# Order of weight turns, stores and the last plain block in a hybrid encoder block (attention, state space layer, two FFNs) on one core

## The chip, the core and the metric

The kernel runs on one core of a Trainium2 chip. Its engines are TensorE (PE, matrix products; PEld is its weight load), VectorE (DVE), ScalarE (ACT), GpSimd (POOL) and SyncE (SP), which here only issues DMAs. The metric is the device time of one execution in microseconds; lower is better.

## The reference

One layer over 1024 tokens of width 1024: a half-weighted SwiGLU FFN, a mixer with neighbourhood attention and a bidirectional state space layer side by side, a second FFN, a gated per-layer embedding and a last norm. All data is float32.

```python
h = h + 0.5 * swiglu(rms_norm(h, ffn1_norm), wg1, wu1, wd1)            # 1024 -> 2816 -> 1024
u = rms_norm(h, mix_norm);  z = u @ w_in                               # q | k | v | s_in | gates
y_attn = neighbourhood_attention(q, k, v, na_rpb) @ w_attn_out         # 8 heads of 64, window 8 x 16
y_ssm = s5_branch(s_in, lam, log_dt, b, c, d, glu_w, glu_b) @ w_ssm_out
g_attn, g_ssm = split(sigmoid(gates), 2)
h = h + (g_attn * y_attn + g_ssm * y_ssm) @ w_out
h = h + 0.5 * swiglu(rms_norm(h, ffn2_norm), ...)
h = h + (p @ w_ple) * sigmoid(rms_norm(h, ple_norm) @ w_ple_gate)
return rms_norm(h, final_norm)

def s5_branch(...):                # 32 groups of 16 channels, 64 complex states each
    y = d_skip * u + scan_forward(u) + scan_backward(u)
    y = gelu(y)
    return y * sigmoid(y @ glu_w + glu_b)
```

## The kernel before

**Products.** Every large product is made of three matmuls on rounded halves: an operand is split into a high part (an ACT cast, L151) and a low part (a DVE subtraction, L152), and `mm3` (L182 to L184) adds high x high, high x low and low x high. Weights come by DMA as 128x512 blocks (`hbuf`, `wblk`, `wgs`), and their split is `wh`, `wl` (in the GLU `wgh`, `wgl`). "Turned" below is said of the attention weights: the scaled scores `sm` are transposed on PE before they meet the values.

**FFN1** uses a scheme of seven products for the four quadrants (class `Seven`). The hidden units are handled in pairs of blocks. Pair 0 is computed plainly (items "C"; matmuls at L657): its four results are evacuated by `evac_plain`, which multiplies by the norm's scale `rs`. The last of them, block 21, is kept back in `late` and finished by `finish_plain`. The pairs 1 to 10 are items ("A", pair, product, gate or up): 7 products x 2, of 12 matmuls each; `evac_a` moves the results `gz`, `uz`, `gx` and so on from PSUM with ACT copies (L577), DVE additions (L581) and an ACT Silu (L585). When a pair has its four blocks, `combine` makes four sums of them (DVE, L534 to L540), and what stage B needs is stored in `a_d`. Stage B, items ("B", product, pair), reads it back as `araw`, splits it into `ah`, `al` and multiplies by `wblk`.

**The side generator.** While FFN1 runs, a generator advances by one tick every three matmuls. `gen_params` loads the parameters of the state space layer (`g_prm`, L775) into the pool `gp` and works them out on DVE. Then for each of 16 pairs of groups `gen_pair` lets POOL build the tables `gm` and `em`, and 25 ticks later `gen_pair_products` turns `gm` on PE (`tp`), multiplies `em` by `bd` (`kp`), copies `kp` into `ka` and stores to DRAM: `fm` to `f_d`, and pieces of `ka` and `em` to `e_d`. `begun` is what opens the way: it ends the hand-written order for DVE and ACT, closes the pool `up` that held the norm's scales, and opens `gp` in its memory.

**The mixer.** After the projections of v, q and k, attention runs in 64 units (8 heads x 2 row blocks x 4 column blocks), one per step `j`. A step computes the scores of unit j (`attn_scores`: PE `s`, DVE addition of the bias table `tb` and row minimum, ACT exponential L1208, DVE reciprocal L1209, ACT scaling L1210), turns the `sm` of unit j-2 (`attn_turn`, PE `pt`, then `pth`, `ptl`) and multiplies unit j-4 by its values (`attn_values`, `O`). Between steps PE works on the gates' projection (`gt`). From step 48 (`SO`) on, one pair of the state space output starts in each step: `ssm_out` loads `emi` from `e_d` and `u_d`, and copies the states into `xs`; three steps later its matmuls `yo` follow. Then comes the GLU: `glu_out(m, t)` for two halves t of the tokens and four blocks m of the weights.

**What sets the order.** The order on PE is written out by hand for the whole kernel, that on DVE and ACT until `begun`. The rest, with POOL and SP, is put in order by a scheduler when the program is built; each engine then works through its queue in order, SP's DMA issues too. Most tiles of 128x512 of the mixer (`sm`, `pth`, `ptl`, `vhl`, `emi`, the GLU's weight halves) share one pool of 56 buffers.

Of the kernel before, what the change touches and what calls it, by code (L numbers as in the profile page):

```python
# [8 lines left out]
F32 = mybir.dt.float32  # L9
# [7 lines left out]
P = 128  # L17
# [4 lines left out]
NH = 8  # L22
GRID = 64
L = 8
NCH = SEQ // L
# [13 lines left out]
def encoder_block(ctx, tc, I, out):  # L39
# [396 lines left out]
    class Ffn:  # L436
# [118 lines left out]
        def evac_plain(self, c, g, o):  # L555
            x, r = self.hid.setdefault(0, {}), self.seven.rs[int(c[0]) - 1]
            if g == 0:
                x[c] = tmp("c" + c)
                V.tensor_tensor(x[c], o, r, ALU.mult)
                A.activation(x[c], x[c], AF.Silu)  # L560
                return
            V.tensor_tensor(x[c], o, x[c], ALU.mult)
            V.tensor_tensor(x[c], x[c], r, ALU.mult)
            if c != "21":
                self.out(0, "a" + c, x[c])
            else:
                self.combine(0, x, tmp("s1"), tmp("s2"), tmp("s4"))

        def evac_a(self, p, i, g):
            z = self.hid.setdefault(p, [{}, {}])[g]  # L570
# [127 lines left out]
        def run(self):  # L698
# [4 lines left out]
            for n, item in enumerate(items):  # L703
# [186 lines left out]
    def gen_pair(pr):  # L890
# [35 lines left out]

        cmul(em, tg, "pe", L + 1, bc, (0, 1))
        load_bc(pr + 1)
        for g in range(2):
            for r in range(2):  # L930
                for d in range(2):
                    n0 = 1 - d
                    nc.sync.dma_start(e_d[2 * pr + g, r * 64:(r + 1) * 64, (1 + d) * P:(2 + d) * P],
                                      em[g * 64:(g + 1) * 64, r, d, n0:n0 + L].rearrange("p n o -> p (n o)"))
# [6 lines left out]
    def gen_pair_products(pr, gm, em, bd):  # L941
# [20 lines left out]
        A.copy(ka[:, 128:240], kp[0:32, 144:256])  # L962
        V.tensor_tensor(ka[:, 112:128], ka[:, 112:128], kp[0:32, 128:144], ALU.add)
        V.scalar_tensor_tensor(ka[:, 112:128], gen["dm"], gen["dk"][:, pr:pr + 1], ka[:, 112:128], ALU.mult, ALU.add)
        for s in range(L):
            nc.sync.dma_start(e_d[2 * pr:2 * pr + 2, s * 16:(s + 1) * 16, 0:P],
                              ka[:, (L - 1 - s) * 16:(L - 1 - s) * 16 + P])


    f_cm = tc.tile_pool(name="f1", bufs=1)  # L970
# [128 lines left out]
    def ssm_out(pr):  # L1099
# [8 lines left out]
        xs = tw("xs", [P, 2, 2, NCH], F32)  # L1108
        for g in range(2):
            for r in range(2):  # L1110
                for d in range(2):
                    sd = Xv[g * 64:(g + 1) * 64, r, pr, d * (NCH + 2):d * (NCH + 2) + NCH]
                    (A.copy if g == r else V.tensor_copy)(xs[r * 64:(r + 1) * 64, g, d], sd)

        def go():
            o = bank("yo")
# [48 lines left out]
    def load_v(hd, cb):  # L1165
# [7 lines left out]
        V.tensor_tensor(hl[0:n, :, 1], vf[0:n], hl[0:n, :, 0].bitcast(F32), ALU.subtract)  # L1173
        vld[hd, cb] = hl

    def make_tabs(hd, rb):
        bt = ap_.tile([P, 12, 32], F32, tag="bt", bufs=1, name="bt")
        e0 = 4 - 4 * rb
        nc.sync.dma_start(bt.rearrange("p r c -> p (r c)"), I["rpbw"][hd, :, e0 * 32:(e0 + 12) * 32])
        row = tmp("row", [P, 12, 32])  # L1180
        V.tensor_tensor(row, bt,
                        rowm[:, rb].unsqueeze(2).broadcast_to([P, 12, 32]), ALU.add)
        res = []
        for v in range(3):
            n, f0 = (24, 32, 24)[v], (8, 0, 0)[v]
            tb = ap_.tile([P, 12, 32], F32, tag="tb", bufs=3, name="tb")
            V.tensor_tensor(tb[:, :, 0:n], row[:, :, f0:f0 + n],
                            colm[:, v, f0:f0 + n].unsqueeze(1).broadcast_to([P, 12, n]), ALU.add)
            res.append(tb)
        tabs[hd, rb] = res  # L1190
# [91 lines left out]
    def mixer_side():  # L1282
# [21 lines left out]
        n = len(units)  # L1304
        for cb in range(4):
            load_v(0, cb)
        make_tabs(0, 0)
        scan_steps(4)
        yield 6
        sms, pts, O = {}, {}, {}  # L1310
        so = {}
        SO = 48
        for j in range(n + 5):
            if j < n:
                hd, rb, cb = units[j]
                while hd not in qkv:
# [1 line left out]
                if cb == 0 and j > 0:  # L1318
                    make_tabs(hd, rb)
                sms[j] = attn_scores(hd, rb, cb)  # L1320
            if 0 <= j - 2 < n:
                pts[j - 2] = attn_turn(units[j - 2][2], sms.pop(j - 2))
            if 0 <= j - 4 < n:
                hd, rb, cb = units[j - 4]
                if cb == 0:
                    O[hd, rb] = bank("O")
                attn_values(hd, rb, cb, O[hd, rb], *pts.pop(j - 4))
                if rb == 1 and hd + 1 < NH:
                    load_v(hd + 1, cb)
            scan_steps(2)  # L1330
            if j >= SO:
# [11 lines left out]
        glu_w(0)  # L1343
        glu_w(1)
        yield 13
        for t in range(2):
            glu_split(t)
# [407 lines left out]
```

## Time and profile before

| | us |
|---|---|
| median of 3 runs | 2137.89 (2136.31 to 2138.95) |
| profiled execution | 2143.67 |
| its span | 2141.9 |
| PE busy | 2100.0 (98%) |
| DVE busy | 1418.3 (66%) |
| ACT busy | 981.7 (46%) |
| POOL busy | 377.6 (18%) |

The mean granted clock of PE over the profiled execution is 0.994. Times in views are microseconds from the start of the span. In a timeline row stand the start, the length, the engine, the line of the kernel, the operation, output and inputs, and in brackets the engine's idle time before it with what ended that. "SPq" is the issue of a DMA on SP. A row of waits gives the time in all, how often, and the longest. A row of windows gives the length of the window, the busy time and number of instructions of PE, PEld, DVE, ACT and POOL, then the granted clock of PE, the mean busy share of the 16 DMA engines and the GB/s that they moved.

### The profile page before, as it was taken

The page shows a single profiled execution, that of the slowest core. Times are in us where ns is not written, and L with a number is a line of the kernel's source. Part 1 is how long each engine was busy: PE and PEld are TensorE (multiplying, and loading weights), DVE is VectorE, ACT ScalarE, POOL GpSimd, SP SyncE. Part 2 cuts the span into 40 slices and gives each one's busy share as a digit, 9 for nine tenths or more (in the row PEclk, how much of TensorE's full clock was granted, in tenths as well). Part 3 has the DMA queues.
Part 4 walks back from the last instruction along what each step waited for, and adds up shares of the span by engine and source line. Part 5 has one row for each costly group of instructions (what it writes and reads, how often), then busy time and mean ns, then how long its engine had stood idle before and what let it go on. Part 6 is the DMA issues. An engine that isn't in the chain of part 4 may idle for free.

```text
span 2141.9 us, 28398 instructions
## 1 busy us (share of the span) xinstructions
PE 2100.0 (98%) x9708; PEld 1720.3 (80%) x9708; DVE 1418.3 (66%) x2452; ACT 981.7 (46%) x1829; POOL 377.6 (18%) x620
## 2 busy tenths in 40 slices
PE   8999999999999999999999999999999999999998
PEld 3787888878888888888888878788888888888886
DVE  7896776667967334677653666896656565785855
ACT  6433333334445334666764522553333333545544
POOL 0026655541000007888000000000000000000000
PEclk9999999999999999999999999999999999999999
DMA  3434433465543552233467731242322328543302
GB/s 131 143 121 134 129 133 114 153 221 199 187 118 109 162 172 67 70 91 95 139 180 246 241 108 65 93 136 100 125 92 100 122 88 284 162 120 95 114 29 79
DMA packets 201105, 282.06 MB, mean 132 GB/s; under 512 B 42624, under 2 KB 85760, under 8 KB 200960
## 3 DMA queue, kind: packets, MB, share of 16 engines
q1 hardware_dynamic: 186112, 259.27, 38.0%
q10 hardware_dynamic: 14848, 20.98, 2.9%
q8 instruction: 76, 1.25, 0.2%
q14 instruction: 69, 0.57, 0.1%
HBM read 197.86 MB, written 82.31 MB: 131 GB/s over the span
## 4 chain that ended last, share of the span: by engine, by line
PE 88%; DMA 4%; DVE 3%; ACT 2%; SPq 1%; issue 1%; POOL 0%; ACTq 0%; DVEq 0%
PE dx L182 4%; PE dx L183 4%; PE dx L184 4%; PE gx L182 3%; PE ux L182 3%; PE gx L183 3%; PE gx L184 3%; PE ux L184 3%; PE ux L183 3%; PE dy L184 2%; PE dy L182 2%; PE dy L183 2%; PE gt L182 2%; PE gt L184 2%; PE gt L183 2%; PE gy L182 2%
## 5 line engine op out<-in xcount | busy, mean ns | idle before, releaser
L151 ACT CAST wh<-hbuf 128x512 fp32r<-128x512 f32 x280 | 173.1, 622 | 403.4 <-PE gx L183 88.0
L152 DVE TENSOR_TENSOR wl<-hbuf,wh 128x512 fp32r<-128x512 f32 x280 | 205.9, 738 | 126.8 <-ACT wh L151 124.5
L151 ACT CAST wh<-wblk 128x512 fp32r<-128x512 f32 x162 | 100.5, 622 | 167.2 <-PE dx L183 71.2
L152 DVE TENSOR_TENSOR al<-araw,ah 128x512 fp32r<-128x512 f32 x154 | 106.9, 697 | 55.2 <-PE dx L183 21.1
L152 DVE TENSOR_TENSOR wl<-wblk,wh 128x512 fp32r<-128x512 f32 x162 | 110.5, 685 | 47.6 <-ACT wh L151 41.5
L182 PE MATMUL dx<-ah,wh 128*128 128x512 f32 x352 | 138.0, 392 | 0.3 <-DVE hbuf L694 0.3
L184 PE MATMUL dx<-ah,wl 128*128 128x512 f32 x352 | 137.0, 389 | 0.0
L183 PE MATMUL dx<-al,wh 128*128 128x512 f32 x352 | 137.0, 389 | 0.0
L1094 POOL TENSOR_TENSOR sc<-X,rho 128x128 f32<-128x128 f32 x128 | 76.8, 600 | 327.6 <-ACT X L1077 317.6
L182 PE MATMUL gx<-xh,wh 128*128 128x512 f32 x320 | 125.8, 393 | 3.8 <-DVE c L581 3.8
L182 PE MATMUL ux<-xh,wh 128*128 128x512 f32 x320 | 125.7, 393 | 2.4 <-DVE c L581 2.3
L183 PE MATMUL gx<-xl,wh 128*128 128x512 f32 x320 | 125.2, 391 | 0.0
L184 PE MATMUL gx<-xh,wl 128*128 128x512 f32 x320 | 125.1, 391 | 0.0
L183 PE MATMUL ux<-xl,wh 128*128 128x512 f32 x320 | 125.0, 391 | 0.0
L184 PE MATMUL ux<-xh,wl 128*128 128x512 f32 x320 | 125.0, 391 | 0.0
L151 ACT CAST ah<-araw 128x512 fp32r<-128x512 f32 x154 | 94.8, 619 | 50.2 <-PE dx L183 12.8
L182 PE MATMUL gt<-xh,wh 128*128 128x512 f32 x256 | 103.8, 405 | 0.0
L184 PE MATMUL gt<-xh,wl 128*128 128x512 f32 x256 | 100.4, 392 | 0.0
L183 PE MATMUL gt<-xl,wh 128*128 128x512 f32 x256 | 100.4, 392 | 0.0
L426 DVE TENSOR_TENSOR hbuf<-hbuf 128x512 f32<-128x512 f32 x120 | 91.4, 763 | 2.0
L182 PEld LDWEIGHTS dx<-ah,wh 128*128 128x128 f32 x352 | 66.1, 188 | 15.0 <-DVE hbuf L694 0.9
L183 PEld LDWEIGHTS dx<-al,wh 128*128 128x128 f32 x352 | 66.1, 188 | 14.1 <-issue 0.5
(376 smaller groups left out, 5728.0 us busy)
## 6 DMA issues: line engine op xcount, KB each, us to landing
araw<-a_d SPq DMA_DIRECT2D x154, 256.0 KB
a_d<-c SPq DMA_DIRECT2D x148, 256.0 KB
wblk<-in_wd SPq DMA_DIRECT2D x88, 256.0 KB
hbuf<-in_wg SPq DMA_DIRECT2D x40, 512.0 KB
hbuf<-in_wu SPq DMA_DIRECT2D x40, 512.0 KB
wst<-in_win SPq DMA_DIRECT2D x26, 512.0 KB
hbuf<-in_xT SPq DMA_DIRECT2D x32, 256.0 KB
h_d<-hbuf ACTq DMA_DIRECT2D x32, 256.0 KB
```

Source lines behind the costliest of these rows:

```text
L151: A.copy(hi, src)
L152: return eng.tensor_tensor(lo, src, hi.bitcast(F32), ALU.subtract)
L182: T.matmul(o, lhsT=wh, rhs=xh, start=first, stop=False, skip_group_check=more)
L183: T.matmul(o, lhsT=wh, rhs=xl, start=False, stop=False, skip_group_check=more)
L184: T.matmul(o, lhsT=wl, rhs=xh, start=False, stop=last, skip_group_check=more)
L426: V.tensor_tensor(b11, (b12, b22, None, None, b21)[i - 2], b11, ALU.subtract)
L1094: G.tensor_tensor(sc, both, rho4, ALU.mult)
```

## The change

It has six parts.

1. The last plain block, 21, is evaluated (`finish_plain`) at item ("A", 1, 3, 0) instead of ("A", 2, 1, 0), and no longer calls `combine` there. `begun` moves from ("A", 2, 1, 0) to ("A", 2, 0, 0). `combine` of pair 0 stays at ("A", 2, 1, 0). The generator waits 10 ticks instead of 6 before its first pair.
2. Each pair's stores to `e_d` are 4 DMAs instead of 16: `em` in two of 64x2x256, `ka` in two of 16x8x128 with overlapping reads.
3. `ssm_out` copies the states into `xs` by four copies of 64 x 256 instead of eight of 64 x 128.
4. The bias table `bt` is loaded one table ahead.
5. Unit j-3 is turned in step j (before j-2), and unit j-5 meets its values (before j-4); there is one step more.
6. The GLU's four weight blocks are loaded and split once, at the steps 64 to 67, and kept for both halves; before, `glu_w` ran eight times, two blocks ahead.

```diff
         def evac_plain(self, c, g, o):
...
             if c != "21":
                 self.out(0, "a" + c, x[c])
-            else:
-                self.combine(0, x, tmp("s1"), tmp("s2"), tmp("s4"))
...
+                if item == ("A", 1, 3, 0):
+                    self.finish_plain()
+                if item == ("A", 2, 0, 0) and self.seven.plain:
+                    self.begun()
                 if item == ("A", 2, 1, 0) and self.seven.plain:
-                    self.finish_plain()
-                    self.begun()
+                    self.combine(0, self.hid[0], tmp("s1"), tmp("s2"), tmp("s4"))
...
         for g in range(2):
-            for r in range(2):
-                for d in range(2):
-                    n0 = 1 - d
-                    nc.sync.dma_start(e_d[2 * pr + g, r * 64:(r + 1) * 64, (1 + d) * P:(2 + d) * P],
-                                      em[g * 64:(g + 1) * 64, r, d, n0:n0 + L].rearrange("p n o -> p (n o)"))
+            ev = em[g * 64:(g + 1) * 64].rearrange("p r d n o -> p r (d n o)")[:, :, 16:16 + 2 * P]
+            nc.sync.dma_start(e_d[2 * pr + g].rearrange("(r p) c -> p r c", r=2)[:, :, P:3 * P], ev)
...
-        for s in range(L):
-            nc.sync.dma_start(e_d[2 * pr:2 * pr + 2, s * 16:(s + 1) * 16, 0:P],
-                              ka[:, (L - 1 - s) * 16:(L - 1 - s) * 16 + P])
+        for g in range(2):
+            k0 = ka[g * 16:(g + 1) * 16, (L - 1) * 16:(L - 1) * 16 + 1]
+            lags = bass.AP(tensor=k0.tensor, offset=k0.offset, ap=[list(k0.ap[0]), [-16, L], [1, P]])
+            nc.sync.dma_start(e_d[2 * pr + g].rearrange("(s i) c -> i s c", s=L)[:, :, 0:P], lags)
...
         yield from gen_params()
         load_bc(0)
-        yield 6
+        yield 10
...
-                for d in range(2):
-                    sd = Xv[g * 64:(g + 1) * 64, r, pr, d * (NCH + 2):d * (NCH + 2) + NCH]
-                    (A.copy if g == r else V.tensor_copy)(xs[r * 64:(r + 1) * 64, g, d], sd)
+                s0 = Xv[g * 64:(g + 1) * 64, r, pr, 0:1]
+                both = bass.AP(tensor=s0.tensor, offset=s0.offset, ap=[list(s0.ap[0]), [NCH + 2, 2], [1, NCH]])
+                (A.copy if g == r else V.tensor_copy)(xs[r * 64:(r + 1) * 64, g], both)
...
     def make_tabs(hd, rb):
-        bt = ap_.tile([P, 12, 32], F32, tag="bt", bufs=1, name="bt")
-        e0 = 4 - 4 * rb
-        nc.sync.dma_start(bt.rearrange("p r c -> p (r c)"), I["rpbw"][hd, :, e0 * 32:(e0 + 12) * 32])
+        b = 2 * hd + rb
         row = tmp("row", [P, 12, 32])
-        V.tensor_tensor(row, bt,
+        V.tensor_tensor(row, bts.pop(b),
                         rowm[:, rb].unsqueeze(2).broadcast_to([P, 12, 32]), ALU.add)
+        load_bias(b + 1)
...
         o = bank("glu")
-        wm = glu["w"].pop(0)
-        if 4 * t + m < 6:
-            glu_w((m + 2) % 4)
+        wm = glu["w"][m]
...
-        for j in range(n + 5):
+        for j in range(n + 6):
...
-            if 0 <= j - 2 < n:
-                pts[j - 2] = attn_turn(units[j - 2][2], sms.pop(j - 2))
-            if 0 <= j - 4 < n:
-                hd, rb, cb = units[j - 4]
+            if 0 <= j - 3 < n:
+                pts[j - 3] = attn_turn(units[j - 3][2], sms.pop(j - 3))
+            if 0 <= j - 5 < n:
+                hd, rb, cb = units[j - 5]
...
+                if NPAIR <= p < NPAIR + 4:
+                    glu_w(p - NPAIR)
```

**ACT while the third pair of FFN1 runs.** Each `wh` is the cast of one item's weights; `c11` copied from `uz` is what DVE adds `ux` to, and `fm` is the first generated pair's store. Before:

```order
L577 COPY c11_1200<-gz_1187 128x512
L151 CAST wh_1274<-hbuf_92 128x512
L151 CAST wh_1294<-hbuf_92 128x512
L151 CAST wh_1313<-hbuf_92 128x512
L585 ACTIVATE c11_1200<-c11_1200 128x512
L151 CAST wh_1333<-hbuf_92 128x512
L151 CAST wh_1352<-hbuf_92 128x512
L151 CAST wh_1398<-hbuf_92 128x512
L577 COPY c11_1251<-uz_1207 128x512
L577 COPY c22_1311<-gy_1298 128x512
```

The same place with the change:

```order
L575 COPY c11_1225<-gz_1187 128x512
L151 CAST wh_1268<-hbuf_92 128x512
L575 COPY c11_1245<-uz_1232 128x512
L151 CAST wh_1288<-hbuf_92 128x512
L583 ACTIVATE c11_1225<-c11_1225 128x512
L151 CAST wh_1307<-hbuf_92 128x512
L151 CAST wh_1327<-hbuf_92 128x512
L575 COPY c22_1305<-gy_1292 128x512
```

The copy of `uz` stood behind six casts after that of `gz`; now it stands behind one.

**SP at the end of stage A.** `bc` is the next pair's coefficients, `hbuf<-in_xT` the input read again for the residual, `x8` a run of eight equal rows. Before:

```order
L607 DMA wblk<-in_wd 128x512 x7
L530 DMA a_d<-c_3941 128x512
L966 DMA e_d<-ka 2x16x128 x8
L888 DMA bc<-in_ssm_bc 128x192
L933 DMA e_d<-em 64x128 x8
L608 DMA araw<-a_d 128x512 x4
```

With the change:

```order
L967 DMA e_d<-ka 16x8x128 x2
L889 DMA bc<-in_ssm_bc 128x192
L980 DMA hbuf<-in_xT 128x512
L605 DMA wblk<-in_wd 128x512
L980 DMA hbuf<-in_xT 128x512
L530 DMA a_d<-c_3779 128x512
L933 DMA e_d<-em 64x2x256 x2
L980 DMA hbuf<-in_xT 128x512
L605 DMA wblk<-in_wd 128x512 x5
L980 DMA hbuf<-in_xT 128x512
L605 DMA wblk<-in_wd 128x512 x2
L606 DMA araw<-a_d 128x512
```

Sixteen stores stood between the last stores of `a_d` and the first reads of `araw`; now four do, and loads of `wblk` and `xT` stand there too.

**PE at the first units of attention.** `s` is the scores of a unit, `pt` a turn, and the number of a tile tells one unit from the next. Before, the first turn follows the third unit's scores:

```order
L1201 MATMUL s_7687<-kh_7478,qs_7370 128x384
L1202 MATMUL s_7687<-kl_7479,qs_7370 128x384
L1217 MATMUL pt_7696<-ident_72,sm_7632 96x128 x3
L182 MATMUL gt_7650<-xh_6496,wh_7317 128x512
L183 MATMUL gt_7650<-xl_6497,wh_7317 128x512
```

With the change:

```order
L1209 MATMUL s_7528<-kh_7286,qs_7178 128x288
L1210 MATMUL s_7528<-kl_7287,qs_7178 128x288
L1225 MATMUL pt_7537<-ident_72,sm_7442 96x128 x3
L182 MATMUL gt_7518<-xh_5853,wh_7357 128x512
L183 MATMUL gt_7518<-xl_5854,wh_7357 128x512
```

The same turn, of the first unit, now follows the fourth unit's scores (128x288), so one unit more lies between a unit's scores and its turn.

More of the change, by code (lines that the diff above doesn't have):

```diff
@@ L1174, in load_v, with load_bias @@
         vld[hd, cb] = hl
+    bts = {}
+    def load_bias(b):
+        if b < 2 * NH:
+            e0 = 4 - 4 * (b % 2)
+            bts[b] = ap_.tile([P, 12, 32], F32, tag="bt", bufs=1, name="bt")
+            nc.sync.dma_start(bts[b].rearrange("p r c -> p (r c)"), I["rpbw"][b // 2, :, e0 * 32:(e0 + 12) * 32])
     def make_tabs(hd, rb):
-        bt = ap_.tile([P, 12, 32], F32, tag="bt", bufs=1, name="bt")
-        e0 = 4 - 4 * rb
-        nc.sync.dma_start(bt.rearrange("p r c -> p (r c)"), I["rpbw"][hd, :, e0 * 32:(e0 + 12) * 32])
+        b = 2 * hd + rb
         row = tmp("row", [P, 12, 32])
-        V.tensor_tensor(row, bt,
+        V.tensor_tensor(row, bts.pop(b),
                         rowm[:, rb].unsqueeze(2).broadcast_to([P, 12, 32]), ALU.add)
+        load_bias(b + 1)
         res = []
@@ L1306, in mixer_side @@
             load_v(0, cb)
+        load_bias(0)
         make_tabs(0, 0)
@@ L1320, in mixer_side @@
                 sms[j] = attn_scores(hd, rb, cb)
-            if 0 <= j - 2 < n:
-                pts[j - 2] = attn_turn(units[j - 2][2], sms.pop(j - 2))
-            if 0 <= j - 4 < n:
-                hd, rb, cb = units[j - 4]
+            if 0 <= j - 3 < n:
+                pts[j - 3] = attn_turn(units[j - 3][2], sms.pop(j - 3))
+            if 0 <= j - 5 < n:
+                hd, rb, cb = units[j - 5]
                 if cb == 0:
                     O[hd, rb] = bank("O")
-                attn_values(hd, rb, cb, O[hd, rb], *pts.pop(j - 4))
+                attn_values(hd, rb, cb, O[hd, rb], *pts.pop(j - 5))
                 if rb == 1 and hd + 1 < NH:
@@ L1342, in mixer_side @@
             glu_load(m)
-        glu_w(0)
-        glu_w(1)
         yield 13
```

## Prediction

> **What bounds the kernel now.** I read the busy line of the page first, then the waits of the tensor engine (PE) over the whole span: what the engine waits for, which engine and line release it, us in all, times, longest.
>
> ```profile
> PE 2100.0 (98%) x9708; PEld 1720.3 (80%) x9708; DVE 1418.3 (66%) x2452; ACT 981.7 (46%) x1829; POOL 377.6 (18%) x620
> ...
> PE pt L1217 <- ACT sm L1210: 6.9, 4, 2.8
> PE g L657 <- ACT xg L346: 6.1, 1, 6.1
> PE gx L182 <- DVE c L581: 3.8, 1, 3.8
> ...
> PE ux L182 <- DVE c L581: 2.3, 1, 2.3
> ...
> PE tp L946 <- POOL gm L923: 1.4, 1, 1.4
> PE glu L182 <- ACT wgh L151: 1.0, 1, 1.0
> ...
> PE kp L957 <- POOL em L923: 0.7, 1, 0.7
> ```
>
> PE is busy for 2100.0 of 2141.9 us, so 41.9 us of waits are all that a better order can win, with the half-clock time that some waits draw behind them. The change leaves PE's work as it is, so the question is which of these rows it reaches. I see four places; the 6.1 us at the start (L657) it doesn't touch.
>
> **Place A, the second and third pair of FFN1: 6.1 us.** The timeline around it, with start, length and, in brackets, the idle time before; then two windows with the granted clock behind POOL's column:
>
> ```profile
> 116.90 0.69 DVE L563 TENSOR_TENSOR c<-c,rs 128x512 f32<-128x512 f32 x1
> 117.67 0.33 SPq L775 DMA_DIRECT2D g_prm<-in_ssm_p  x1
> 149.32 2.35 POOL L903 TENSOR_TENSOR bb<-g_fr,bc 128x64 f32<-128x64 f32 x1 [26.89 <-DVE g_fr L836]
> 166.44 1.40 POOL L923 TENSOR_TENSOR em<-em,tg 128x576 f32<-128x576 f32 x1
> 160.97 0.62 ACT L151 CAST wh<-hbuf 128x512 fp32r<-128x512 f32 x1 [2.10 <-PE gx L183]
> 161.49 0.58 ACT L577 COPY c<-uz 128x512 f32<-128x512 f32 x1
> 162.69 0.68 DVE L581 TENSOR_TENSOR c<-ux,c 128x512 f32<-128x512 f32 x1
> 167.89 1.29 PE L957 MATMUL kp<-em,bd 128*32 128x128 f32 x8 [0.70 <-POOL em L923]
> 168.00:172.00 4.00, 4.00 (x15) 3.04 (x15) 0.38 (x2) 0.75 (x3) 3.94 (x10) 0.57 0.36 107
> ```
>
> ACT works its queue in order, and the copy of `uz` stands behind a row of weight casts, each of which waits for PE: 2.10 us idle and 0.62 us of work, 2.72 us, the length of one item of 12 matmuls. So the copy runs at 161.49, DVE's sum at 162.69, and PE waits 2.3 us. With the change's order the copy stands behind the first cast after `gz`, five casts or 13.6 us earlier, so at about 148: this wait goes, with more than 10 us to spare.
>
> The waits for `gm` and `em` (1.4 and 0.7) belong to the first pair of the state space layer. Its parameter load leaves at 117.67, right behind the product with `rs` at 116.90, the last reader of the memory it needs. The change makes that product ten items earlier: 10 x 2.72 = 27.2 us, so near 90. What it costs: PE turns and multiplies this pair 12 matmuls (2.72 us) sooner, since the wait of 10 ticks for 6 doesn't quite use up the two items by which `begun` is moved (8 ticks). `em` is done at 167.84, while PE, which takes it up at 167.89, would want it near 160.7 (less the waits of 0.7, 1.4 and 2.3 and one item of 2.72): POOL has to be 7.1 us ahead of before. It starts when DVE's parameter chain ends, which now can begin up to 27.2 us earlier. I take both waits as gone.
>
> Then the clock: in 168 to 172 PE was granted 0.57, so 4.00 x 0.43 = 1.72 us were lost behind these waits. Sum of A: 2.3 + 1.4 + 0.7 + 1.7 = 6.1. Moving the four additions and stores of pair 0 relative to the evacuation costs DVE nothing new: the same instructions, spread over more time.
>
> **Place B, stage A's end: 5.4 us.** SP's queue, a piece of the chain that ended last (the DMA row), and windows:
>
> ```profile
> 456.36 5.42 SPq L966 DMA_DIRECT2D e_d<-ka  x8
> 462.33 5.13 SPq L933 DMA_DIRECT2D e_d<-em  x8
> 467.51 1.99 SPq L608 DMA_DIRECT2D araw<-a_d  x4
> 468.60 4.93 DMA araw<-a_d
> 761.73 3.65 SPq L1375 DMA_DIRECT2D u_d<-su  x8
> 464.00:468.00 4.00, 4.00 (x19) 3.33 (x18) 1.68 (x3) 1.10 (x3) 3.10 (x6) 1.00 0.23 51
> 472.00:476.00 4.00, 0.39 (x1) 0.37 (x2) 3.34 (x6) 1.75 (x4) 0.00 (x0) 0.97 1.01 360
> 476.00:480.00 4.00, 4.00 (x12) 3.12 (x11) 2.05 (x4) 0.73 (x2) 0.00 (x0) 0.60 1.05 406
> ```
>
> Sixteen small stores hold SP for 5.42 + 5.13 = 10.6 us, and the reads of `araw` that stage B starts from are queued behind them. The third issued lands at 473.53; its cast and DVE's work behind it release PE after 3.8 us. Four stores cost 4 x 0.46 = 1.8 us by the `u_d` row (3.65 / 8, the same 16x8x128 shape as the new `ka` store), 2.6 us by the present `em` row (5.13 / 8): SP is freed of about 8 us. The new order spends part of it on weight and xT loads placed ahead of `araw`: six to eight at 0.46 us, some 3 us. That leaves 5 us, so `araw` leaves near 463 to 464 and lands by 470, against a need 3.8 us before 473.5. The bounds: 0 if the DMA engines set the landing (1.01 busy in 472 to 476), the whole 3.8 if SP does. The row nearest in time to the new issue, 464 to 468, has the engines at 0.23, so I take 3.8. The clock of 0.60 behind it gives 4.00 x 0.40 = 1.6. The 15 other pairs shorten SP's queue too, but no PE wait names them: nothing.
>
> **Place C, attention beside the state space output: 10.3 us.** ACT's waits between 1020 and 1110, four turns on PE, and windows:
>
> ```profile
> ACT vhl L1172 <- DMA vf<-v_d: 6.5, 3, 2.5
> ACT sm L1210 <- DVE stat L1209: 5.4, 8, 2.5
> ...
> ACT xs L1113 <- PE yo L1121: 2.8, 1, 2.8
> 1051.42 0.55 PE L1217 MATMUL pt<-ident,sm 128*128 128x128 f32 x3 [2.76 <-ACT sm L1210]
> 1063.98 0.53 PE L1217 MATMUL pt<-ident,sm 128*96 128x128 f32 x3 [1.54 <-ACT sm L1210]
> 1105.24 0.49 PE L1217 MATMUL pt<-ident,sm 128*96 128x128 f32 x3
> 1109.74 0.49 PE L1217 MATMUL pt<-ident,sm 128*128 128x128 f32 x3
> 1048.00:1052.00 4.00, 1.24 (x10) 0.96 (x9) 1.35 (x4) 3.85 (x9) 0.00 (x0) 1.00 0.66 191
> 1052.00:1056.00 4.00, 4.00 (x22) 3.71 (x21) 2.49 (x6) 1.49 (x4) 0.00 (x0) 0.58 0.68 198
> 1064.00:1068.00 4.00, 4.00 (x29) 3.68 (x30) 2.62 (x10) 3.73 (x12) 0.00 (x0) 1.00 0.76 243
> 1100.00:1104.00 4.00, 4.00 (x18) 3.58 (x18) 2.92 (x8) 2.50 (x7) 0.00 (x0) 0.57 0.86 259
> ```
>
> The scaled scores `sm` come late because ACT is held up in its queue by copies for `vhl` and `xs`. The turn one step later gives `sm` one step more: 1109.74 - 1105.24 = 4.5 us. The longest wait is 2.8, so all four (6.9) go, unless the hold-ups grow. The values move a step too, so pth and ptl keep their two steps. Two of the waits drew a half clock behind them (1052 and 1100: 1.68 + 1.72 = 3.4); behind the 1.54 us wait the slice 1064 to 1068 shows 1.00. The larger `xs` copies, two on ACT and two on DVE for four and four, and the earlier bias load shorten the queues; priced at nothing, they are covered by the same step. Sum: 6.9 + 3.4 = 10.3.
>
> **Place D, the GLU: 1.0 us.** The end of the chain there:
>
> ```profile
> 1144.26 7.12 DMA hbuf<-h_d
> 1151.40 5.27 DMA wgs<-in_wglu
> ```
>
> A weight fetched for the second half lands at 1156.67 behind reads of `h`, and PE waits 1.0 us for its cast. Now all four are split once, during the last attention steps, and kept. The four loads, casts and subtractions that go were hidden otherwise; those that come earlier lie beside the last steps of attention.
>
> **Sum:** 6.1 + 5.4 + 10.3 + 1.0 = 22.8 us. A wait removed usually leaves a shorter one: for the four places I keep 0.5 us each, near the smallest of these rows (0.7), so 2.0 us. That is -20.8 against the profiled execution, 2143.67 to 2122.9. The profiled execution lies 5.8 us above the median of the runs, 2137.89; taken as an offset that stays, the median goes to 2117.1.
>
> **Rivals.**
>
> 1. B stays: once issued earlier, more reads meet the wblk traffic and the engines (1.01 and 1.05 busy) set the landing. Against it: 0.23 busy just before. Price 5.4: 2122.5. Chance 0.12.
>
> 2. C is won half: ACT's hold-ups (6.5 and 2.8 us in the rows above) come in series, and with a step of slack the queue drifts on until the turn waits again. For it: the same few causes delay `sm` step after step. Price half of 10.3, some 5: 2122. Chance 0.14.
>
> 3. The half clock isn't drawn by these short waits, and stays when they go. Against it: 0.58 stands right behind a slice in which PE worked 1.24 of 4 us, and 1.00 behind the shorter 1.54 us wait. Then A's 1.7 and C's 3.4 are not won: 2122.2. Chance 0.04. [...]
>
> 4. The parameter chain on DVE delays work of the first generated pairs, or ends less than 7.1 us earlier, and A is lost: price 6.1, 2123.2. For it: the 31.6 us between the load and POOL's first use were DVE's, whose queue is shared with the weights. Chance 0.05.
>
> 5. Slower: the pool of 512-wide buffers runs out. `sm` lives a step longer, and four pairs of GLU weights are held at the end; a load of `emi` without a buffer then stops SP's whole queue, with the `v` and weight loads behind it. SP now issues these loads without a break:
>
> ```profile
> 1062.47 0.40 SPq L1104 DMA_DIRECT2D emi<-e_d  x1
> ...
> 1070.44 0.42 SPq L1105 DMA_DIRECT2D emi<-u_d  x1
> ```
>
> Sixteen such loads in 8 us speak against it: buffers are free. A stop would last up to one step, 4.5 us, half of it on average, 2.2 us; at 16 pairs that is +35 us, 2152. It decides from 16 x 1.6 us on (20.8 + 4.3 = 25.1). Chance 0.08, half of it reaching that point.
>
> That the change doesn't reach these rows is excluded by the order of the instructions in A, B and C; only times are open.
>
> **How the numbers follow.** The forecast holds 0.57, the rivals 0.12, 0.14, 0.04, 0.05, 0.08. Predicted 2117. A difference of 0.2%, 4.3 us, is about what a measurement here tells from no change: faster is below 2133.6. Low end: no residue (2115.1), and another 5.8 us if the offset of the profiled execution lay in waits that go too: 2109. High end: two of rivals 1 to 4 together, 2127 to 2128, taken to 2129; outside are three at once and rival 5. Faster 0.92 (forecast and rivals 1 to 4), same 0.04 and slower 0.04 (the two halves of rival 5).
>
> **What would show it.** PE's waits should have no row for `ux`/`tp`/`kp` near 160, none for `gx` near 472, none for `pt`, none for `glu` on a weight, and the four slices at 0.57 to 0.60 should read 1.00. SP should spend 2 to 3 us a pair on `e_d`. Wrong would be: PE waiting on DVE or ACT between 90 and 150 (A's cost), `gx` still released by `araw`, new waits at `pt` or `O`, PE waiting for `emi` at `yo`, or `glu` waiting for `yl`, the splits now that the weights are there.

## Result and the profile after

The changed kernel takes 2118.78 us (median of 5 runs, 2116.55 to 2119.36), the kernel before 2138.88 beside it: a ratio of 0.9906 with a 95% interval of 0.9892 to 0.9921, so 20.1 us less. The forecast was 2117 us, 20.8 less. The profiled execution took 2118.57 us, with a span of 2116.8 and a mean clock of 0.997.

PE's busy time on the page, and its waits over the whole span, in the changed kernel:

```profile
PE 2089.2 (99%) x9708; PEld 1716.0 (81%) x9708; DVE 1416.2 (67%) x2416; ACT 978.3 (46%) x1793; POOL 387.3 (18%) x620
```

```profile
PE g L655 <- ACT xg L346: 6.1, 1, 6.1
PE ms L241 <- DVE acc L225: 3.5, 2, 2.7
PE g L183 <- DVE xl L152: 2.2, 3, 0.9
PE yo L1119 <- DVE ot L1244: 1.8, 1, 1.8
PE ms L243 <- ACT sq L218: 1.4, 1, 1.4
PE dn L182 <- ACT mh L151: 1.4, 1, 1.4
PE gx L182 <- DVE c L579: 1.2, 1, 1.2
```

The rows of `pt`, `ux`, `tp`, `kp` and `glu` are gone. The row at `gx` isn't the old one: it lies at 99 us, not at 476. Two waits are new, then: 1.2 us at `gx` and 1.8 us at `yo`.

**Place A.** From the timeline of the changed kernel:

```profile
89.45 0.69 DVE L563 TENSOR_TENSOR c<-c,rs 128x512 f32<-128x512 f32 x1
90.20 0.34 SPq L776 DMA_DIRECT2D g_prm<-in_ssm_p  x1
132.61 0.30 POOL L904 TENSOR_TENSOR bb<-g_fr,bc 128x64 f32<-128x64 f32 x1 [38.08 <-DVE g_fr L837]
149.15 0.58 ACT L575 COPY c<-uz 128x512 f32<-128x512 f32 x1
155.62 1.88 POOL L924 TENSOR_TENSOR em<-em,tg 128x576 f32<-128x576 f32 x1
160.85 0.60 PE L945 MATMUL tp<-ident,gm 128*128 128x128 f32 x4
```

The product with `rs` runs at 89.45 (before 116.90), the parameters are fetched at 90.20 (117.67), and `em` is done at 157.50, 3.3 us before PE begins with this pair. Of the 27 us by which the chain starts earlier, DVE and POOL turn 10.3 into an earlier `em`; 7.1 were needed.

**Place B.** SP's queue in the changed kernel:

```profile
444.74 2.25 SPq L967 DMA_DIRECT2D e_d<-ka  x2
450.33 1.28 SPq L933 DMA_DIRECT2D e_d<-em  x2
456.96 0.39 SPq L606 DMA_DIRECT2D araw<-a_d  x1
461.21 1.67 SPq L606 DMA_DIRECT2D araw<-a_d  x3
```

The stores take 3.5 us for 10.6, dearer one by one than the `u_d` row had suggested (0.9 us for 0.46). Only the first read of `araw` leaves much earlier: PE is 6.0 us further on here than before at the same point, so 456.96 corresponds to 463.0 (before 467.51), but the next three, from 461.21, to 467.2 and later (468.1). What else changed is DVE's queue. Before:

```profile
474.26 0.69 DVE L152 TENSOR_TENSOR al<-araw,ah 128x512 fp32r<-128x512 f32 x1 [0.66 <-ACT ah L151]
474.87 0.68 DVE L581 TENSOR_TENSOR c<-gx,c 128x512 f32<-128x512 f32 x1
```

and in the changed kernel, with the casts of its second and third `araw`:

```profile
463.90 0.69 DVE L152 TENSOR_TENSOR al<-araw,ah 128x512 fp32r<-128x512 f32 x1 [1.53 <-ACT ah L151]
464.51 0.69 DVE L579 TENSOR_TENSOR c<-gx,c 128x512 f32<-128x512 f32 x1
...
467.29 0.69 DVE L152 TENSOR_TENSOR al<-araw,ah 128x512 fp32r<-128x512 f32 x1 [1.50 <-ACT ah L151]
466.64 1.36 ACT L151 CAST ah<-araw 128x512 fp32r<-128x512 f32 x2 [0.77 <-DMA araw<-a_d]
```

The sum for which PE waited stood behind the low halves of three `araw`; now it stands behind that of one.

**Clock.** The windows of the changed kernel at the old places read 1.00; one later slice, behind the 1.41 us wait at `dn`, does not, as it didn't before:

```profile
160.00:164.00 4.00, 4.00 (x24) 3.17 (x23) 3.96 (x6) 2.95 (x9) 3.91 (x5) 1.00 0.39 132
464.00:468.00 4.00, 4.00 (x20) 3.30 (x19) 2.50 (x5) 2.27 (x5) 0.00 (x0) 1.00 1.05 389
472.00:476.00 4.00, 4.00 (x20) 3.17 (x19) 2.82 (x5) 1.17 (x4) 4.00 (x5) 1.00 0.96 361
1044.00:1048.00 4.00, 4.00 (x31) 3.67 (x30) 0.51 (x2) 2.05 (x6) 0.00 (x0) 1.00 0.93 274
1212.00:1216.00 4.00, 4.00 (x13) 3.11 (x13) 2.99 (x5) 0.58 (x2) 0.00 (x0) 0.63 0.51 150
```

**A ledger.** PE runs the same matmuls in nearly the same order in every kernel here, so two traces can be compared by when the same matmul starts. The table gives, for each stretch of the program, how many us longer a kernel takes than the changed kernel's profile takes for it (one profiled execution each; worked out from PE's timelines). The stretches are named by the changed kernel's times: the first pairs of FFN1 (79 to 148), place A (148 to 190), place B (437 to 534), the steady part of attention (810 to 1014), places C and D together (1014 to 1170), and what follows up to FFN2 (1170 to 1401).

| kernel | 79-148 | A | B | 810-1014 | C and D | 1170-1401 |
|---|---|---|---|---|---|---|
| before | -1.4 | 6.6 | 5.3 | 1.6 | 10.0 | 1.6 |
| changed, without part 1 | -1.3 | 6.7 | 1.1 | 0.0 | 0.6 | -3.2 |
| changed, 16 stores | 0.0 | 0.0 | 3.7 | 0.0 | -0.2 | -3.2 |
| changed, turn at j-2 | 0.0 | 0.0 | -0.4 | 1.5 | 5.5 | -1.5 |
| changed, GLU weights as before | 0.0 | 0.0 | 0.3 | 0.0 | 2.2 | -3.2 |
| changed, without parts 3 to 5 | 0.0 | 0.0 | -0.1 | 1.5 | 5.5 | -3.2 |
| before with part 1 | 0.0 | 0.0 | 4.2 | 1.5 | 7.5 | -1.5 |
| before with the 4 stores | -1.4 | 6.8 | 0.9 | 1.4 | 4.6 | -1.6 |
| before with parts 3 and 4 | -1.3 | 5.0 | 4.7 | 1.7 | 7.8 | 0.1 |
| before with the turn at j-3 | -1.4 | 6.4 | 6.7 | 0.0 | -0.7 | -1.6 |
| changed, once more | 0.0 | 0.0 | -0.4 | 0.0 | 2.4 | -3.2 |
| changed, `ys` in the larger pool | 0.0 | 0.0 | 0.3 | 0.0 | 0.0 | -3.2 |
| the same, the last product with `rs` on POOL | 0.0 | 0.0 | -0.2 | 0.0 | -0.7 | -1.6 |

The before row, with 0.7 us at the `v` projection and some tenths elsewhere, adds up to the 25.1 us by which the two spans differ. That is 5 more than the runs' 20.1: before's profiled execution, 2143.67, lies above every one of its timed runs (2132.44 to 2142.84).

### The profile page after: what moved, and what is told of

Read it like the earlier page. It is cut to its first block, busy times and chain, and to the rows that moved or that the text cites. A ratio compares the mean times of both kernels' runs of the same rounds, so it can differ in the third digit from the quotient of the medians.

```text
span 2116.8 us, 28037 instructions
## 1 busy us (share of the span) xinstructions
PE 2089.2 (99%) x9708; PEld 1716.0 (81%) x9708; DVE 1416.2 (67%) x2416; ACT 978.3 (46%) x1793; POOL 387.3 (18%) x620
## 4 chain that ended last, share of the span: by engine, by line
PE 90%; DVE 5%; ACT 2%; DMA 1%; issue 1%; SPq 0%; DVEq 0%; ACTq 0%
PE dx L182 4%; PE dx L183 4%; PE dx L184 4%; PE ux L182 3%; PE gx L182 3%; PE ux L183 3%; PE ux L184 3%; PE gx L184 3%; PE gx L183 3%; PE gt L182 3%; PE gt L183 3%; PE gt L184 3%; PE dy L183 2%; PE dy L182 2%; PE dy L184 2%; PE uy L182 2%
## 5 line engine op out<-in xcount | busy, mean ns | idle before, releaser
L152 DVE TENSOR_TENSOR wl<-hbuf,wh 128x512 fp32r<-128x512 f32 x280 | 210.5, 754 | 124.3 <-ACT wh L151 122.0
```

The lines of the kernel that those rows point to most:

```text
L152: return eng.tensor_tensor(lo, src, hi.bitcast(F32), ALU.subtract)
```

## Experiments

**What each part is worth when it alone is undone.** Part 1 undone (begun, the last plain block and the ticks as before):

```diff
-                if item == ("A", 1, 3, 0):
-                    self.finish_plain()
-                if item == ("A", 2, 0, 0) and self.seven.plain:
-                    self.begun()
+                if item == ("A", 2, 1, 0) and self.seven.plain:
+                    self.finish_plain()
+                    self.begun()
...
-        yield 10
+        yield 6
```

> The changed kernel with part 1 alone undone (last plain block, begun and the 10 ticks as before). Theory: place A stands by itself. The ledger of the two traces has the changed kernel 1.4 us behind at 104 us (a new wait of PE on DVE, 1.21) and 6.6 ahead from there to 192, net 5.3; so this kernel should be 5.3 us slower than the changed one (about 2124), with the rows ux on c (2.3), tp on gm (1.4) and kp on em (0.7) back and the 1.21 at gx near 99 gone. Rival: the parts interact through the scheduler, and the ux wait goes for another reason (fewer DMAs in the program); then less than 2.5 us slower and no ux row.

2122.41 us (2121.59 to 2125.57; ratio to before 0.9925, 0.9913 to 0.9938), 3.6 above the changed kernel's median, 4.3 above that of its second set of runs. Its waits:

```profile
PE ux L182 <- DVE c L581: 2.9, 2, 2.3
...
PE tp L944 <- POOL gm L923: 1.2, 1, 1.2
...
PE gx L182 <- DVE c L581: 0.3, 1, 0.3
```

The old waits are back (`kp` with 0.2 us only), and that at 99 us is gone. In the ledger place A and the stretch before it make 5.4, as forecast; another 1.1 lies at place B. The rival falls.

The 16 stores back, all else changed:

> The changed kernel with the 16 stores per pair back, all else changed. Theory: SP's queue is the limit at the end of stage A; the wait of gx on c near 470 (3.8) and its half clock (1.6 to 1.7) come back: 5.3 us slower, about 2124. Rival: the loads moved by the earlier begun, not the stores, took the wait away; then within 1.5 us of the changed kernel and no wait near 470. A second rival: 192 more DMAs slow other places too; then more than 7 us slower.

2119.77 us (2119.00 to 2122.39; 0.9916, 0.9902 to 0.9929): 1.0 and 1.6 above the changed kernel. PE's idle times by the timeline:

```profile
465.66 0.50 PE L182 MATMUL gx<-xh,wh 128*128 128x512 f32 x1 [0.60 <-DVE c L579]
484.39 0.50 PE L182 MATMUL dz<-ah,wh 128*128 128x512 f32 x1 [0.43 <-ACT ah L151]
489.05 0.50 PE L182 MATMUL dz<-ah,wh 128*128 128x512 f32 x1 [1.00 <-ACT ah L151]
```

and its SP queue:

```profile
483.95 3.05 SPq L967 DMA_DIRECT2D e_d<-ka  x5
487.05 0.41 SPq L606 DMA_DIRECT2D araw<-a_d  x1
487.56 4.97 SPq L934 DMA_DIRECT2D e_d<-em  x8
```

The stall comes back, 3.7 us in the ledger, but not in one piece: with part 1 the order of the loads is another, the stores that hold up an `araw` are now those of the next pair, and none of the short waits has a half clock behind it. SP's queue as the cause holds. The runs show less than these 3.7 us. In the profiles they are taken back elsewhere: against the changed kernel's first profile by 3.2 us behind 1170, against its second by 2.6 us around `yo`, where the wait is 1.3 us here and no low clock follows.

The turn at j-2 and the values at j-4, the other parts kept:

> The changed kernel with the turn at j-2 and the values at j-4 again, the larger xs copies and the earlier bias load kept. Theory: the step of slack took the waits away; pt on sm comes back with 4 or so waits, 6.9 us, and two half clocks, 3.4, while the new 1.8 at yo goes: 8.5 us slower, about 2127. Rival: the smaller number of xs copies (2 for 4 on each engine) had already taken away half of the hold-up; then 3 to 5 us slower, with pt waits of 2 to 4 us in all and one half clock or none.

2119.90 us (2118.61 to 2123.42, 4 runs; 0.9914, 0.9900 to 0.9927). The profiled execution is the slowest of the four; it has the forecast waits, three for four, and one half clock behind them for two:

```profile
PE pt L1225 <- ACT sm L1218: 5.4, 3, 2.2
```

The median, 1.1 and 1.8 us above the changed kernel, lies below even the rival's range. By itself this run would have said that the turn hardly counts.

The GLU's weights loaded eight times again:

> The changed kernel with the GLU weights loaded eight times again. Theory: the wait of 1.0 us at glu and its slow start come back, 1.5 us slower (2120), which is hardly more than the runs scatter. Rival: the earlier arrival at the GLU, or a different order of the reads of h ahead of the weight, changes the wait; from 0 to 4 us.

2118.07 us (2116.79 to 2120.54; 0.9904, 0.9891 to 0.9918): no difference, and no row of `glu` among PE's waits. Part 6 isn't needed for that wait to go. It may be enough, though: in the two profiles with part 6 and without the later turn (the run before this one and the next) the row is missing too.

**Groups of parts, and parts alone.** The changed kernel without parts 3, 4 and 5:

> The changed kernel with all of the attention side undone: xs in eight copies, the bias table loaded when needed, the turn at j-2 and the values at j-4. Theory now, after the turn alone cost little when undone: the turn's step and the fewer xs copies are substitutes, either covers most of the hold-up on ACT. Then this kernel loses what place C was forecast to give, about 8.5 us against the changed kernel (2127), and its pt waits are longer than those with the turn alone undone (5.4 us in three). Rival: the waits at pt scatter from execution to execution, and the size of place C in the profile of before (6.9 and two half clocks) was a high draw; then 2 to 4 us, as with the turn alone undone.

2125.53 us (2122.30 to 2126.42; 0.9934, 0.9921 to 0.9947): 6.8 and 7.4 above the changed kernel, near the theory. Its profile, though, shows about what the kernel with only the turn undone showed:

```profile
PE pt L1217 <- ACT sm L1210: 6.1, 4, 2.6
```

The kernel before with part 1 alone:

> The kernel before with part 1 alone (last plain block, begun, 10 ticks). Theory: place A stands by itself: 5.3 us faster than before (2133), as the ledger of the two traces has it, and the waits at gx near 470 and at pt stay as they were. Rival: undone from the changed kernel it cost 3.6 to 4.6 us, and alone it gives that, 4 us; a second rival: the later loads of stage A move with it (bc, xT, wblk stand elsewhere in SP's queue), and the wait near 470 shrinks too: 8 us or more.

2128.16 us (2125.79 to 2130.77; 0.9950, 0.9937 to 0.9964): 9.9 less, the second rival's number. The ledger gives 6.6 - 1.4 + 1.1 = 6.3 of it to places A and B; the row at `gx` near 467 is down to 1.7 us. The other 3 to 4 us are none of part 1's own places. The granted clock of its runs points to fewer half clocks: 0.9962 in the mean, for 0.9939 before, makes an estimated 4.9 us (0.0023 of 2130, from clocks given to three places), of which place A has 1.7; where the others lie isn't shown.

The kernel before with the four stores alone:

> The kernel before with the four stores per pair alone. Theory: the wait of 3.8 us near 470 and its half clock go, 5.3 us faster (2133). Rival: undoing the stores in the changed kernel brought back only small waits at gx and dz, 2.7 us in all and no half clock, since part 1 also moved SP's queue; if SP's time for the stores is only part of the cause here too, 2.5 to 3.5 us faster.

2131.91 us (2129.24 to 2134.00; 0.9967, 0.9956 to 0.9979): 6.1 less, the theory's 5.3 within the interval. At 475 a rest of 0.59 us is left of the 3.8:

```profile
475.38 0.50 PE L182 MATMUL ux<-xh,wh 128*128 128x512 f32 x1 [0.59 <-DVE c L581]
```

DVE's queue is that of the changed kernel here: the sum stands behind one `al`. Place B is 0.9 us with the stores alone, 4.2 with part 1 alone, 3.7 in the changed kernel with 16 stores, and 5.3 with neither (4.7 and 6.7 in the two later kernels with neither): by these profiles the stores are worth 3.7 to 4.4 of the 5.3, part 1 about 1.

The changed kernel once more, beside these:

> The changed kernel once more, as it is. It stands beside the others on the same chip, and shows which small waits in its profile come and go: the 1.2 us at gx near 99 and the 1.8 us at yo near 1041 should come back, the order of the queues being fixed; the 2.7 us at ms near 1360 and the first microseconds may differ by 1 to 2 us. Time within 1.5 us of 2118.8.

2118.14 us (2117.33 to 2118.89; 0.9904, 0.9888 to 0.9919). The 1.2 us at `gx` and the wait at `yo` (2.0 us) are back; behind the latter PE's clock is low this time (rows of windows, two at `yo` and two at `dn`), where the first profile had 1.00 throughout:

```profile
1039.13:1042.54 3.41, 1.40 (x14) 1.26 (x13) 3.41 (x9) 1.15 (x3) 0.00 (x0) 1.00 0.66 212
1042.54:1045.95 3.41, 3.41 (x14) 3.02 (x14) 1.24 (x6) 2.42 (x7) 0.00 (x0) 0.50 0.62 137
1209.80:1213.21 3.41, 2.00 (x10) 1.34 (x8) 2.60 (x5) 0.86 (x2) 0.00 (x0) 1.00 0.44 154
1213.21:1216.62 3.41, 3.19 (x14) 2.38 (x14) 2.58 (x5) 1.86 (x4) 0.00 (x0) 1.00 0.25 78
```

And behind the 1.41 us at `dn` (1213) the clock isn't low here. Once, for 0.6 us, PE waits at `yo` for an `emi`, which the first profile doesn't have.

The kernel before with parts 3 and 4 alone:

> The kernel before with parts 3 and 4 alone: xs in four copies, the bias table loaded one ahead; the turn stays at j-2. Theory: these shorten the queues of ACT and DVE, and are worth about as much as the runs with parts 3 to 5 undone (2125.5) and with the turn alone undone (2119.9) lie apart: 4 to 5 us faster than before. Rival: the profiles of those two kernels show the same waits at pt (6.1 and 5.4 us), so the difference was scatter between batches, and this kernel is within 1.5 us of before.

2135.68 us (2131.25 to 2137.50, 11 runs; 0.9986, 0.9977 to 0.9995): 1.8 less, between theory and rival and nearer the rival.

The kernel before with the later turn alone:

> The kernel before with the turn at j-3 and the values at j-5 alone. Theory: the step of slack by itself takes the pt waits away (6 to 7 us in the profiles that have the turn at j-2) and the 1.5 us that the traces lose between 810 and 1014 in steps too small for the list of waits; with the xs copies still eight, a wait at yo of 2 us stays: 6 to 8 us faster than before (2131). Rival: it needs the smaller xs copies to work, since ACT and DVE stay behind; then 2 to 3 us faster, with pt waits left.

2128.02 us (2126.16 to 2129.63; 0.9952, 0.9939 to 0.9964): 9.5 less, more than expected. In its profile no row of `pt` and none of `glu` is left, only this of the attention side:

```profile
PE yo L1119 <- ACT sm L1210: 1.0, 1, 1.0
...
PE yo L1119 <- DMA emi<-u_d: 0.2, 1, 0.2
```

The step of slack does the whole of place C, and D's wait goes with it, without part 6.

**The new waits.** The changed kernel's timeline around the one at `yo`:

```profile
1037.59 0.56 DVE L1188 TENSOR_TENSOR row<-bt,rowm 128x384 f32<-128x384 f32 x1 [2.34 <-DMA y_d<-ys]
1039.80 1.21 DVE L152 TENSOR_TENSOR wl<-wst,wh 128x1024 fp32r<-128x1024 f32 x1
1040.93 0.67 DVE L1244 TENSOR_TENSOR ot<-O,ol 64x512 f32<-64x512 f32 x1
1041.66 0.49 PE L1119 MATMUL yo<-emi 128*128 128x128 f32 x2 [1.81 <-DVE ot L1244]
```

The chain of waits names the store that `row` waits for:

```profile
1033.65 3.86 DMA y_d<-ys
```

DVE stands for 2.34 us at `row`: its tile comes from a pool of four that `ys` shares, and `row` begins at 1037.59, when the store of a `ys` has landed (1033.65 + 3.86 = 1037.51). `ot`, queued behind, holds the PSUM bank that PE wants: it ends at 1041.60, and PE goes on at 1041.66. So:

```diff
-            ys = tmp("ys", [P, 2, NCH])
+            ys = thid("ys", [P, 2, NCH], F32)
```

> The changed kernel with the tile ys taken from the pool of 56 buffers instead of the pool of four that row, vf, ot and ol share. Theory: PE's new wait at yo near 1041 (1.8 to 2.0 us on DVE's ot) comes from DVE's queue standing still 2.3 us at row until the store of ys to y_d has left one of the four buffers; with ys elsewhere it goes, with the half clock behind it where there is one: 2 to 3.5 us faster than the changed kernel (2118.4), near 2115.5. Rival: row then waits for another of the four (vf or ot, whose stores also take microseconds), and the wait stays within 0.5 us.

2115.52 us (2114.66 to 2116.44; 0.9895, 0.9881 to 0.9908): 3.3 and 2.6 below the changed kernel's two medians, and every run below every one of its nine. They come from different sets of runs, though; measured from the kernel before beside each, it is 22.0 us less against 20.1 and 19.9, so some 2 us. The wait on `ot` is gone; two others of half its length stand in its place:

```profile
PE pt L1225 <- ACT gs L1365: 0.9, 1, 0.9
PE yo L1119 <- ACT ys L1123: 0.9, 1, 0.9
```

By the ledger, places C and D take as long as in the changed kernel's first profile and 2.4 us less than in its second, so the size of the gain rests on the runs; this profile's lead over the first lies behind 1170, where no low clock stands in it.

With, in addition, the last product with `rs` on POOL:

```diff
-            V.tensor_tensor(x[c], x[c], r, ALU.mult)
+            (V if c != "21" else G).tensor_tensor(x[c], x[c], r, ALU.mult)
```

> The same, and the last product of the plain block 21 with rs done on POOL instead of DVE. Theory: the wait of 1.2 us at gx near 99 comes from the 1.38 us that the two operations of the last plain block add to DVE's queue ahead of the weights' preparation; half of it moved to POOL takes 0.7 to 1.2 us from that wait: 1 us faster than with ys alone. Rival: POOL is slower at it and the memory of rs comes free later, which moves g_prm and the parameter chain; DVE's waits on it then cost as much as is won.

2115.34 us (2114.19 to 2115.83; 0.9893, 0.9880 to 0.9907): the same as with `ys` alone. The wait at `gx` is still 1.2 us, and the timeline shows the rival:

```profile
88.94 1.68 POOL L563 TENSOR_TENSOR c<-c,rs 128x512 f32<-128x512 f32 x1 [88.49 <-DVE c L562]
```

```profile
92.81 0.18 DVE L757 TENSOR_SCALAR g_prm<-g_prm 128x32 f32<-128x32 f32 x1 [0.96 <-DMA g_prm<-in_ssm_p]
```

POOL takes 1.68 us for what DVE did in 0.69, the parameters come later, and DVE, on which the first operations on `g_prm` stand ahead of a weight's low half, waits 0.96 us for them.

**Which waits draw a low clock.** Before the last microseconds, every low stretch of PE's clock in the fourteen profiles is at 0.50 and lasts 3.41 us, in four cases twice that, so 1.71 us are lost in each 3.41 (3.41 x 0.50). They start on a grid that runs on through the execution: in before's profile at 168.58, 475.78, 1052.63, 1100.42, 1236.95 and 1387.14, which are 90, 169, 14, 40 and 44 steps of 3.413 us apart. Windows cut along this grid show how a wait falls into the stretches. In the second profile (rows above) the wait at `yo` lies within one stretch; in the first a line of the grid cuts it in two, and the wait at `dn` with the 0.23 us behind it lies in one:

```profile
1037.44:1040.85 3.41, 2.41 (x17) 2.02 (x15) 3.26 (x7) 1.31 (x3) 0.00 (x0) 1.00 0.51 162
1040.85:1044.26 3.41, 2.60 (x18) 2.39 (x19) 2.68 (x9) 1.81 (x6) 0.00 (x0) 1.00 0.54 144
1208.11:1211.52 3.41, 1.77 (x7) 0.96 (x6) 2.30 (x4) 1.65 (x4) 0.00 (x0) 1.00 0.45 154
1211.52:1214.93 3.41, 3.41 (x9) 2.62 (x9) 1.92 (x4) 1.06 (x3) 0.00 (x0) 0.50 0.32 91
```

PE's idle time in a stretch is its length less PE's busy time: 1.00 and 0.81 us around `yo` here, 2.01 in the second profile; 1.64 at `dn` here, 1.41 in the second. In all fourteen profiles, between 60 and 2100 us, a stretch at full clock with 1.99 us or more of idle time was followed by a low one in all of 21 cases, one with less than 1.6 in none, and of the 18 between in 11. In before's profile the five of the first kind have 2.07, 3.24, 2.20, 1.99 and 2.66 us (from 165.17, 472.37, 1049.22, 1097.01 and 1383.73); of its two between, 1.74 us (from 161.76) had 1.00 behind it and 1.63 (from 1233.54) 0.50. The 1.54 us wait before the change with 1.00 behind it (1062.44 to 1063.98) is cut too, into 0.43 and 1.11.

## Why the prediction was right, and where not

The total was right to 1.8 us. At the places A to D together the ledger has 20.5 us, where the sum with its residue had 20.8. That the median agrees as well is in part luck, since the step from the profile to the median failed: "taken as an offset that stays". Before's profile lay 5.8 us above its median; the changed kernel's, 2118.57, lies 0.2 us below. The offset went, and 4.6 us of the 25.1 between the two profiles lie outside A to D (1.6 in the steady part of attention, 1.6 behind 1170, the rest in small pieces). By its steps:

- **Place A, 6.1.** Both mechanisms are shown: undoing part 1 brings the three rows back, and the ledger has 6.4 to 6.8 us for the place in the kernels without part 1, and 5.0 in the one in which no low clock follows. The step that failed is "Moving the four additions and stores of pair 0 relative to the evacuation costs DVE nothing new": the last block's two operations and the first ones of the parameter chain now stand in the stretch from 88 to 93 us, ahead of DVE's preparation of weights, and PE loses 1.4 us at 99. That leaves 5.3. It was rival 4 in small: the chain does delay the weights, at less than a quarter of the price given.
- **Place B, 5.4.** 5.3 in the ledger, and the stores hold it, as the runs with 4 and with 16 show. The step that failed is the one on the way: "`araw` leaves near 463 to 464 and lands by 470" holds for the first read alone. The third lands about as late as before (the second of the two casts from 466.64 begins near 467.3, which corresponds to 473.3; before, 473.61), with the DMA engines at 1.05 in 464 to 468, so there rival 1 saw rightly. It doesn't matter any more, since the scheduler, with SP's queue free, spread the reads and put DVE's sum behind the first. That it is the order on DVE and not the earlier first read is read from the traces and wasn't tried apart. A good 1 us of the 5.3 comes from part 1, and a store's price was half of what it measured.
- **Place C, 10.3.** The later turn alone gave 9.5 us by the runs (7.7 to 13.0 by the ends of its interval, of 2137.47), and its trace has none of the `pt` waits. That sum holds two errors that offset each other. The clock term was too large: of the kernels with the turn at j-2 only before's profile shows two half clocks, the others one or none. And a term was missing: in the steady part of attention, 810 to 1014, each kernel with the turn at j-2 takes 1.4 to 1.7 us longer, in steps too small for the list of waits. In the whole change a wait at `yo` takes back 1.8 to 2.0 us, and 1.7 more where a low clock follows; the residue kept for the four places together was 2.0. Rival 2, half of C lost, saw that a wait would come back here, but not which: not `sm` again, but DVE's wait for a buffer that a store holds.
- **Place D, 1.0.** The wait went, but not only for the reason given: it is gone with the turn alone, without part 6, and it is gone with part 6 and the turn at j-2, beside parts 1 and 2. Part 6 alone wasn't run; on top of the turn it gained nothing that the runs show.
- **Rival 3, the clock.** The rival was wrong, and the forecast right in the sum: the four low stretches priced are gone in both profiles of the changed kernel, 4 x 1.71 = 6.8 us for 6.7. But a wait of this length has no fixed price: behind the same 1.41 us wait at `dn` a low clock stands in the first profile (0.50, behind a stretch of the grid with 1.64 us of idle time) and not in the second (1.00, behind one with 1.41), and at `yo` the second profile has a new one, behind a stretch with 2.01.
- **Rival 5, the buffers.** No wait shows that the pool of 56 ran out; the sign named for it, PE waiting for `emi` at `yo`, is 0.6 us once in the second profile. The pool of four did run out, at `ys`.

**What the sum hides.** The parts aren't additive. Alone, part 1, the stores, the turn, and parts 3 and 4 gave 9.9, 6.1, 9.5 and 1.8, 27 in all against 20 for the whole. Undone one at a time, part 1, the stores, the turn and the GLU cost 4.0, 1.3, 1.4 and -0.4 (means over the changed kernel's two medians). Two causes are seen in the traces: the new wait at `yo` (1.0 us with the turn alone, 1.8 to 2.0 in the changed kernel, with or without a low clock behind it) gives part of the gain back when all parts are there; and place C itself goes up and down with what comes ahead of it. With nothing of C changed, that stretch was 10.0 in before's profile, 7.5 with part 1 and 4.6 with the stores; two, one and no low stretch lie in it, which is 3.4 of the 5.4 us between them. So part of what part 1 and the stores gave alone was place C, which the turn then removed anyway. That this is the whole of the difference isn't shown: it would need more than one profile of each kernel. Open too is why the kernel with the turn alone undone ran at 2119.9 and that with parts 3 to 5 undone at 2125.5, when their profiles agree and parts 3 and 4 alone gave 1.8. The agreement says little, as the two profiles are the slowest of four runs (2123.42) and the fastest of five (2122.30). The runs' granted clocks, 0.9970 and 0.9956 in the mean, would make some 3 of the 5.6 us (an estimate, 0.0014 of 2120, from clocks given to three places).

## What to carry to other kernels

Read a gain from several places as a sum only while the places don't feed each other: here the stretch of place C went from 10.0 us to 7.5 with part 1 alone and to 4.6 with the stores alone, though nothing of C had changed. One more step between producer and consumer took away the four waits at `pt` here (6.9 us; 9.5 by the runs), which no single transfer explains, but look afterwards at which in-order queue now waits for a buffer; here a store of 3.9 us held one of four tiles, and giving that tile to a larger pool was worth another 2 to 3 us by the runs. Price a clock loss behind a wait of some 1.5 to 2 us as a chance: here each low stretch cost 1.71 us, and whether it came went with how much of the wait fell into one stretch of a grid of 3.413 us (in 21 of 21 cases with 1.99 us or more of idle time, in 11 of 18 with 1.6 to less than that); the place of that grid differed between two executions of one program.

## What the runs showed of the hardware

PE's granted clock went to 0.50 for stretches of 3.41 us, on a grid of 3.413 us whose place differed between the changed kernel's two profiles by half a step (low from 1211.52 in the first, lines at 1209.80 and 1213.21 in the second). In the fourteen profiles, between 60 and 2100 us, a stretch with 1.99 us or more of idle PE time was followed by a low one each time (21 cases), one with less than 1.6 us never. Waits of 1.4 to 2.7 us were followed by a low clock in some executions and not in others: behind the 1.41 us at `dn` 0.50 in one profile of the changed kernel and 1.00 in the other; behind the wait at `yo` 1.00 (1.8 us) and 0.50 (2.0 us); behind the 2.7 us at `ms` 0.50 in the changed kernel's first profile and 1.00 in that with `ys` in the larger pool.

In the ledger's last column the low stretch at `dn`, and a second place of the same size at the norm, `ms`, make three levels 1.6 us apart for programs that don't differ there: 0.0 with both (the changed kernel's first profile, low from 1211.52 and from 1361.70), -1.6 with the one at the norm alone (the last product on POOL) and -3.2 with neither (`ys` in the larger pool). Before's 1.6 has both too, and 1.0 us more of waits at `dn` (2.6 for 1.6 us). The two profiles of the changed kernel, one program, differ by 3.2 us in that column.
